# Expert weights of a routed FFN loaded, split and released in half chunks, with six half buffers for three whole ones

## The chip, the cores and the metric

The kernel runs on one core of a Trainium2 chip, as one program. The metric is the time of one execution on the device in microseconds, the median of several runs. The engines are named as the profile names them: PE is TensorE (PEld its weight loads), DVE is VectorE, ACT is ScalarE, POOL is GpSimd, SP is SyncE, which here only issues DMAs.

## What is computed

One layer of an encoder on 1024 tokens of width 1024, all in float32: a mixing sub-layer (a Fourier branch and attention, gated and projected), then a feed-forward sub-layer in which a router sends each token to 4 of 32 experts, each with a normalising residual. The change lies in the second sub-layer. Cut to what matters, the reference does this there:

```python
logits = xf @ w_router + b_router                   # 1024 tokens, 32 experts
top_vals, top_idx = lax.top_k(logits, 4)
top_w = softmax(top_vals)
# for each expert e and each of its tokens:
h = xb @ w_gate_up[e] + b_gate_up[e]                # 1024 -> 2048
gate = minimum(h[:, :1024], 7.0); up = clip(h[:, 1024:], -7.0, 7.0)
act = (up + 1.0) * gate * sigmoid(1.702 * gate)
y = act @ w_down[e] + b_down[e]                     # 1024 -> 1024
# y times the token's weight is added to the token's row of the output
```

The weights of the 32 experts, 12 MiB each, are read once.

## The kernel before

Up to about 1047 us of the profile the kernel computes the mixing sub-layer, the norm and the router, and ranks the experts by their number of tokens. The expert stage then works through all 32 experts by rank. Each rank has a fixed capacity in tokens (CAPS, from 416 down to 64); tokens beyond it would go through a loop at the end (the pool `pvw`), which uses the same loader.

Float32 products are made of float32r matmuls: a weight is split into `whi`, its rounded value (ACT, line 147), and `wlo`, the rest (DVE, line 148), and the tokens' values are split the same way. A product takes three matmuls (hi by hi, lo by hi, hi by lo), or two where the tokens' two parts lie side by side in one matmul.

**Chunks.** An expert's weights come in 12 chunks of 1 MiB: eight of gate and up (`G1`, chunks 0 to 7: four groups of 256 columns of each, in two halves of the contraction) and four of down (`G2`, chunks 8 to 11). `load_chunk` (line 994) takes a `wraw` tile of 128 x 2048 floats, lets SP issue its loads (two DMAs of 512 KB for gate and up, line 1003; one of 1 MiB for down, line 1005 for experts with few tokens, 1007 for the popular ones), and splits the tile in two halves of 1024 columns (`HALVES`, line 1012) into one `whi` and one `wlo` tile. The pool `pew` has three buffers of each kind. `Stream.get` hands out the next chunk and asks for loads two chunks ahead.

**Lanes.** The 14 popular ranks (over 128 tokens) form lane a, the other 18 lane b. `moe_plan` merges the steps of both lanes into one list by a cost of each step and a rest behind some, and the program is written out in this order; the framework then builds every engine's queue from it ahead of the run with a simulated timeline, so matmuls of neighbouring steps may be interleaved, and the queues are then fixed.

- Lane a keeps weights as the stationary operand (`cols`, line 1108 and on): a pair of chunks (h = 0, 1) fills four PSUM tiles `psg`, indexed by j (128 columns of the group) and t (gate or up). For each of the four in turn the k steps of the chunk run (lines 1124 to 1128). After the second chunk each j is evicted (`gu`, lines 1137 to 1141), put through the activation (lines 1143 to 1146), and split into `aTa` (lines 1152 and 1153), the moving operand of the down chunks (`down_mm`, lines 1203 and 1204, or the three of `mm3`, lines 141 to 143). Results are weighted (`weigh`, line 1215) and scattered to the tokens' rows by POOL.
- Lane b keeps the tokens stationary (`rows`, lines 1164 to 1169): a pair of chunks accumulates into one PSUM tile `psr`; the result is turned (`at`, line 1189) for the down chunks.

While an expert runs, POOL gathers the rows of the next expert of its lane, and PE turns them (line 1088) in between its down chunks; the table of rows that the gather needs is loaded by SP during the second chunk. The first steps also add the down bias to the output (`bias_out`, lines 1256 to 1259).

Of the kernel before, what the change touches and what calls it, by code (L numbers as in the profile page):

```python
# [12 lines left out]
F32 = mybir.dt.float32  # L13
# [10 lines left out]
P = 128  # L24
# [13 lines left out]
CAPS = [416, 320, 288, 288, 256, 256, 240, 208, 208, 192, 192, 160, 160, 160] + 7 * [128] + 11 * [64]  # L38

RANK_AT = 6  # L40
HALVES = [(0, 4), (4, 8)]
N_BIG = sum(n > P for n in CAPS)
LANE_A = [9, 0, 4, 1, 5, 2, 6, 3, 7, 8, 10, 11, 12, 13]
LANE_B = list(range(NE - 1, N_BIG - 1, -1))
# [62 lines left out]
def layer_kernel(ctx, tc, x, c, w_ada, b_ada, w_in, q_norm_g, k_norm_g, w_fourier, w_attn_o, w_out,  # L107
# [886 lines left out]
    def load_chunk(pl, wgu, wdn, i, wide=True, after=None):  # L994


        raw = pl.tile([P, KT, 256], F32, name="wraw")
        c, h = divmod(i % 8, 2)
        ks = slice(4 * h, 4 * h + 4)
        if i in G1:  # L1000
            rv = raw.rearrange("p (k t) f -> p k t f", t=2)
            for t in range(2):
                sp.dma_start(rv[:, :, t, :], wgu[:, ks, t, c * 256:(c + 1) * 256])
        elif wide:
            sp.dma_start(raw.rearrange("p (k t) f -> p k (t f)", t=2), wdn[:, ks, c * 512:(c + 1) * 512])
        else:
            sp.dma_start(raw, wdn[:, :, (i - 8) * 256:(i - 7) * 256])
        hi = pl.tile([P, KT, 256], F32R, name="whi")
        lo = pl.tile([P, KT, 256], F32R, name="wlo")
        with tc.issue_after(after.ins) if after else nullcontext():  # L1010
            for a, b in HALVES:
                split(raw[:, a:b, :], hi[:, a:b, :], lo[:, a:b, :])
        if i in G1 or wide:
            return tuple(w.rearrange("p (k t) f -> p k (t f)", t=2) for w in (hi, lo))
        return hi, lo

    def weights_of(e):
        return (w_gate_up[0][bass.ds(e, 1)].rearrange("o (k p) (t f) -> p (o k) t f", p=P, t=2),
# [8 lines left out]
        vec.tensor_tensor(a_, a_, gu[:n, 1, :], op=ALU.mult)  # L1027

    plan = moe_plan()
    with tc.tile_pool(name="pew", bufs=3, side=RIGHT) as pew, tc.tile_pool(name="pes", bufs=1, side=RIGHT) as pes, \  # L1030
# [27 lines left out]
        class Expert:  # L1058
# [49 lines left out]
            def cols(self, i):  # L1108

                n, xT, aT, r = self.n, self.xT, self.aT, self.r  # L1110
                merged = n < 256
                c, h = divmod(i, 2)
                wh, wl = wst.get()
                if h == 0:
                    self.pg = [[peg.tile([P, 512], F32, name="psg") for t in range(2)] for j in range(2)]
                for j in range(2):
                    for t in range(2):
                        ps = self.pg[j][t]
                        cs = slice(t * 256 + j * P, t * 256 + (j + 1) * P)
                        for k in range(4):  # L1120
                            first, last = h == 0 and k == 0, h == 1 and k == 3
                            xh, xl = xT[:, 4 * h + k, 0, :], xT[:, 4 * h + k, 1, :]
                            if merged:
                                pe_.matmul(ps[:, :2 * n], wh[:, k, cs], xT[:, 4 * h + k, :, :], start=first, stop=False)  # L1124
                            else:
                                pe_.matmul(ps[:, :n], wh[:, k, cs], xh, start=first, stop=False)  # L1126
                                pe_.matmul(ps[:, :n], wh[:, k, cs], xl, start=False, stop=False)  # L1127
                            pe_.matmul(ps[:, :n], wl[:, k, cs], xh, start=False, stop=last)  # L1128
                    if h == 0:
                        continue  # L1130
                    ft = 2 * c + j
                    gu = pe.tile([P, 2, n], F32, name="gu", bufs=1)
                    for t, lim in ((0, LIMIT), (1, LIMIT + 1.0)):
                        ps = self.pg[j][t]
                        bb = BG[:, 8 * t + ft, r:r + 1]
                        if merged:
                            act.activation(gu[:, t, :], ps[:, n:2 * n], AF.Identity, bias=bb)
                            vec.tensor_tensor(gu[:, t, :], ps[:, :n], gu[:, t, :], op=ALU.add)
                            vec.tensor_scalar(gu[:, t, :], gu[:, t, :], lim, None, op0=ALU.min)
                        else:  # L1140
                            vec.tensor_scalar(gu[:, t, :], ps[:, :n], bb, lim, op0=ALU.add, op1=ALU.min)
                    sg = pe.tile([P, n], F32, name="sgg", bufs=1)
                    act.activation(sg, gu[:, 0, :], AF.Sigmoid, scale=SLOPE)
                    vec.scalar_tensor_tensor(gu[:, 1, :], gu[:, 1, :], 1.0 - LIMIT, gu[:, 0, :], op0=ALU.max,
                                             op1=ALU.mult)
                    vec.tensor_tensor(sg, gu[:, 1, :], sg, op=ALU.mult)
                    nf = n // P
                    for b0, nb_, m in ((0, nf, P), (nf * P, 1, n - nf * P)):
                        if nb_ and m:
                            av = aT[:, ft, 2 * b0:2 * (b0 + nb_ * m)].rearrange("p (b t q) -> p b t q", b=nb_, t=2)  # L1150
                            sv = sg[:, b0:b0 + nb_ * m].rearrange("p (b q) -> p b q", b=nb_)
                            act.activation(av[:, :, 0, :], sv, AF.Copy)  # L1152
                            vec.tensor_tensor(av[:, :, 1, :], sv, f32(av)[:, :, 0, :], op=ALU.subtract)  # L1153

            def rows(self, i):
# [5 lines left out]
                wh, wl = wst.get()  # L1161
                o = self.ps[:m, :]
                if h == 0:
                    pe_.matmul(o, self.sel[:, :m], b2v[:, :, c * 256:(c + 1) * 256], start=True, stop=False)
                for k in range(4):
                    xk, last = xT[:, 4 * h + k, :, :], h == 1 and k == 3
                    if m > n:
                        pe_.matmul(o, xk, wh[:, k, :], start=False, stop=False)  # L1168
                        pe_.matmul(o, xk, wl[:, k, :], start=False, stop=last)  # L1169
                    else:  # L1170
                        mm3(o, xk[:, 0, :], xk[:, 1, :], wh[:, k, :], wl[:, k, :], False, last)
                if h == 0:
                    return
                pv = self.ps.rearrange("p (t f) -> p t f", t=2)
# [18 lines left out]
            def down_mm(self, o, b0, m, w, k0, first, last):  # L1193

                aT = self.aT
                wh, wl = w
                hs, ls = slice(2 * b0, 2 * b0 + m), slice(2 * b0 + m, 2 * (b0 + m))
                bs = slice(2 * b0, 2 * (b0 + m))
                nk = wh.shape[1]
                for k in range(nk):  # L1200
                    f_, l_ = first and k == 0, last and k == nk - 1
                    if m in (32, 64):
                        pe_.matmul(o[:2 * m], aT[:, k0 + k, bs], wh[:, k, :], start=f_, stop=False)
                        pe_.matmul(o[:2 * m], aT[:, k0 + k, bs], wl[:, k, :], start=False, stop=l_)
                    else:
                        mm3(o[:m], aT[:, k0 + k, hs], aT[:, k0 + k, ls], wh[:, k, :], wl[:, k, :], f_, l_)

            def weigh(self, o, m, wt, y, cs):

# [127 lines left out]
                e.chunk(i, [partial(nx.xt, *bh) for bh in halves])  # L1337


    with tc.tile_pool(name="pv", bufs=1) as pv, tc.tile_pool(name="pvw", bufs=3) as pvw, \  # L1340
            tc.tile_pool(name="pvp", bufs=2, space=PSUM) as pvp:
        nov = nc.values_load(novi[0:1, 0:1], min_val=0, max_val=NB_MAX)
        with tc.For_i(0, nov, 1) as bi:  # L1343
# [32 lines left out]
            for c in range(4):  # L1376
                ps = pvp.tile([P, 512], F32, name="vps")
                pe_.matmul(ps, eb, b2v[:, :, c * 256:(c + 1) * 256], start=True, stop=False)
                for h in range(2):
                    wh, wl = ws3.get()  # L1380
                    for k in range(4):
                        xk = xT[:, 4 * h + k, :, :]
                        mm3(ps, xk[:, 0, :], xk[:, 1, :], wh[:, k, :], wl[:, k, :], False, h == 1 and k == 3)
                gu = pv.tile([P, 2, 256], F32, name="vgu", bufs=2)
                swiglu(gu, ps.rearrange("p (t f) -> p t f", t=2), P, av[:, c * 256:(c + 1) * 256])
            aT = columns(av, "vaT")
            y = pv.tile([P, D], F32, name="vy")
            for c in range(2):
                ps = pvp.tile([P, 512], F32, name="vps")
                for h in range(2):  # L1390
                    wh, wl = ws3.get()
                    for k in range(4):
                        ak = aT[:, 4 * h + k, :, :]
                        mm3(ps, ak[:, 0, :], ak[:, 1, :], wh[:, k, :], wl[:, k, :], h == 0 and k == 0,
                            h == 1 and k == 3)
# [85 lines left out]
```

## Time and profile before

| | |
|---|---|
| median of 3 runs | 2810.29 us (2807.48 to 2818.73) |
| the profiled execution | 2809.73 us |
| its span, first to last instruction | 2808.0 us |
| mean granted TensorE clock | 0.952 of full |
| PE busy (x instructions) | 2544.5 us, 91% (x15948) |
| DVE busy | 2083.0 us, 74% (x3672) |
| ACT busy | 1421.8 us, 51% (x2190) |
| POOL busy | 380.1 us, 14% (x283) |
| moved by DMA | 561.23 MB, mean 200 GB/s |

Busy shares over the whole span are a mean over stages that differ: the expert stage takes from 1047 to 2740 us. The rows further down are from this stage. A group's row gives the instructions of one line and tile: their busy time, the mean of one in ns, and behind the bar the idle time of the engine just ahead of them with what ended it. Matmuls are pipelined, so the mean of one is longer than the step from one to the next. The duration of an SP row is that of issuing, not of the transfer.

### The profile page before, as it was taken

Reading aid. Unit: us, or ns where it says so; the run is one execution under the profiler, and the core shown is the slowest. Engines: PE = TensorE matmul, PEld = TensorE weight load, DVE = VectorE, ACT = ScalarE, POOL = GpSimd, SP = SyncE. Lnnn points to the kernel's source line nnn. Section 1 sums busy time; section 2 is a strip of 40 time slices with the busy share of each in tenths; the row PEclk is TensorE's granted clock in tenths of the full one; section 3 lists DMA queues with packets and bytes.
Section 4 is the critical chain, followed back from the end, with each engine's and each line's share of the span. In section 5 each row is a group of like instructions: output and inputs, shape, how many; then the busy total and the mean of one; then the engine's idle time right before and its main releaser. Section 6 shows DMA issues by size and latency. Waiting matters only on the chain. (4 is left out here: it accounts for less than half of the span.)

```text
span 2808.0 us, 43022 instructions
## 1 busy us (share of the span) xinstructions
PE 2544.5 (91%) x15948; PEld 2307.1 (82%) x15948; DVE 2083.0 (74%) x3672; ACT 1421.8 (51%) x2190; POOL 380.1 (14%) x283
## 2 busy tenths in 40 slices
PE   6999999899999947889989989989999999998991
PEld 5888899799888946789889888977888888897881
DVE  7543438777755956868788888969896888887885
ACT  3411122466621535645566556647665665665562
POOL 3100012211032232000201010011101010020003
PEclk9999999999999958999999999999999999999996
DMA  6154411000054349857889799978988898988774
GB/s 229 55 185 158 160 55 31 16 1 1 1 179 145 121 150 259 250 173 251 255 273 290 239 292 282 301 230 276 287 282 247 273 295 272 290 285 257 248 250 152
DMA packets 468742, 561.23 MB, mean 200 GB/s; under 512 B 26632, under 2 KB 404944, under 8 KB 468480
## 3 DMA queue, kind: packets, MB, share of 16 engines
q1 hardware_dynamic: 448672, 494.41, 53.9%
q0 software_dynamic: 18768, 59.64, 8.4%
q10 hardware_dynamic: 1088, 4.39, 0.5%
q8 instruction: 127, 2.08, 0.3%
q14 instruction: 87, 0.71, 0.1%
HBM read 512.90 MB, written 46.82 MB: 199 GB/s over the span
## 5 line engine op out<-in xcount | busy, mean ns | idle before, releaser
L148 DVE TENSOR_TENSOR wlo<-wraw,whi 128x1024 fp32r<-128x1024 f32 x768 | 909.7, 1217 | 220.1 <-ACT whi L147 216.0
L147 ACT ACTIVATE whi<-wraw 128x1024 fp32r<-128x1024 f32 x768 | 767.9, 1051 | 462.8 <-DMA wraw<-in_w_gate_up_dram 130.7
L1128 PE MATMUL psg<-xTa,wlo 128*128 128x160 f32 (+7 forms) x1792 | 469.5, 278 | 3.1 <-DVE wlo L148 3.0
L1128 PEld LDWEIGHTS psg<-xTa,wlo 128*128 128x128 f32 x1792 | 341.6, 194 | 8.4 <-DVE wlo L148 6.1
L1124 PE MATMUL psg<-xTa,whi 128*128 128x320 f32 (+3 forms) x1024 | 307.1, 367 | 12.4 <-ACT whi L147 10.7
L141 PE MATMUL psd<-whi,aTa 128*128 128x256 f32 (+2 forms) x768 | 220.6, 291 | 27.1 <-ACT aTa L1152 17.6
L1126 PE MATMUL psg<-xTa,whi 128*128 128x256 f32 (+3 forms) x768 | 233.3, 308 | 11.3 <-ACT whi L147 9.1
L1127 PE MATMUL psg<-xTa,whi 128*128 128x256 f32 (+3 forms) x768 | 231.9, 305 | 0.0
L143 PE MATMUL psd<-whi,aTa 128*128 128x256 f32 (+2 forms) x768 | 216.8, 287 | 3.5 <-DVE aTa L1153 3.3
L142 PE MATMUL psd<-wlo,aTa 128*128 128x256 f32 (+2 forms) x768 | 217.5, 285 | 0.1
L1124 PEld LDWEIGHTS psg<-xTa,whi 128*128 128x128 f32 x1024 | 195.8, 194 | 23.5 <-ACT whi L147 13.2
L141 PEld LDWEIGHTS psd<-whi,aTa 128*128 128x128 f32 (+2 forms) x768 | 145.7, 190 | 36.1 <-ACT aTa L1152 21.2
L1126 PEld LDWEIGHTS psg<-xTa,whi 128*128 128x128 f32 x768 | 147.4, 192 | 14.9 <-ACT whi L147 10.8
L991 POOL DMA_INDIRECT acc_d<-xya,tab x33 | 60.6, 1836 | 654.0 <-DVE xya L1215 544.2
L143 PEld LDWEIGHTS psd<-whi,aTa 128*128 128x128 f32 (+2 forms) x768 | 145.0, 190 | 5.0 <-DVE aTa L1153 4.4
L1127 PEld LDWEIGHTS psg<-xTa,whi 128*128 128x128 f32 x768 | 147.5, 192 | 1.3
L1169 PE MATMUL psr<-wlo,xTb 128*128 128x512 f32 x352 | 145.1, 412 | 3.2 <-DVE wlo L148 3.1
L142 PEld LDWEIGHTS psd<-wlo,aTa 128*128 128x128 f32 (+2 forms) x768 | 145.9, 190 | 1.3 <-DVE wlo L148 0.4
L1168 PE MATMUL psr<-whi,xTb 128*128 128x512 f32 x352 | 144.6, 411 | 2.4 <-ACT whi L147 2.4
L147 ACT ACTIVATE wh<-wraw 128x1024 fp32r<-128x1024 f32 (+1 forms) x35 | 48.1, 1377 | 154.4 <-PE psg L206 92.9
L152 ACT ACTIVATE pth<-pst 128x512 fp32r<-128x512 f32 x128 | 75.1, 599 | 86.4 <-PE pst L632 85.1
L141 PE MATMUL pz<-wh,uh 128*128 128x256 f32 x384 | 110.4, 288 | 2.4 <-DVE mrow L480 2.4
(455 smaller groups left out, 6407.5 us busy)
## 6 DMA issues: line engine op xcount, KB each, us to landing
wraw<-in_w_gate_up_dram SPq DMA_DIRECT2D x512, 512.0 KB
wraw<-in_w_down_dram SPq DMA_DIRECT2D x128, 1024.0 KB
wa<-in_w_ada_dram SPq DMA_DIRECT2D x24, 1024.0 KB
wraw<-in_w_in_dram SPq DMA_DIRECT2D x13, 1024.0 KB
xs<-in_x_dram SPq DMA_DIRECT2D x8, 512.0 KB
m_d<-sgm POOLq DMA_DIRECT2D x8, 512.0 KB, 4.1
sa_d<-sgm POOLq DMA_DIRECT2D x8, 512.0 KB, 2.9
wraw<-in_w_attn_o_dram SPq DMA_DIRECT2D x8, 512.0 KB
```

The costliest lines, as they stand in the source:

```text
L141: pe_.matmul(o, lh, rh, start=start, stop=False)
L142: pe_.matmul(o, lh, rl, start=False, stop=False)
L143: pe_.matmul(o, ll, rh, start=False, stop=stop)
L147: act.activation(hi, raw, AF.Copy)
L148: (lo_eng or vec).tensor_tensor(lo, raw, f32(hi), op=ALU.subtract)
L152: act.activation(hi, ps, AF.Copy)
L1124: pe_.matmul(ps[:, :2 * n], wh[:, k, cs], xT[:, 4 * h + k, :, :], start=first, stop=False)
L1126: pe_.matmul(ps[:, :n], wh[:, k, cs], xh, start=first, stop=False)
L1127: pe_.matmul(ps[:, :n], wh[:, k, cs], xl, start=False, stop=False)
L1128: pe_.matmul(ps[:, :n], wl[:, k, cs], xh, start=False, stop=last)
L1168: pe_.matmul(o, xk, wh[:, k, :], start=False, stop=False)
L1169: pe_.matmul(o, xk, wl[:, k, :], start=False, stop=last)
```

## The change

`load_chunk` now makes two half chunks of a chunk. Each has its own `wraw`, `whi` and `wlo` tile of 128 x 1024 floats, its own loads (of two k steps of gate and up, or of half the rows of a down chunk) and its own split, and the pool has six buffers of each kind, so that the bytes stay the same. A chunk is now a list of two pairs. `rows`, `down_mm` and the overflow loop index the right half for each k; their order of matmuls is the same. `cols` runs both k steps of the first half for all four `psg` tiles, then those of the second; the evictions follow after all of it.

```diff
     def load_chunk(pl, wgu, wdn, i, wide=True, after=None):
-        raw = pl.tile([P, KT, 256], F32, name="wraw")
         c, h = divmod(i % 8, 2)
-        ks = slice(4 * h, 4 * h + 4)
-        if i in G1:
-            rv = raw.rearrange("p (k t) f -> p k t f", t=2)
-            for t in range(2):
-                sp.dma_start(rv[:, :, t, :], wgu[:, ks, t, c * 256:(c + 1) * 256])
-        elif wide:
-            sp.dma_start(raw.rearrange("p (k t) f -> p k (t f)", t=2), wdn[:, ks, c * 512:(c + 1) * 512])
-        else:
-            sp.dma_start(raw, wdn[:, :, (i - 8) * 256:(i - 7) * 256])
-        hi = pl.tile([P, KT, 256], F32R, name="whi")
-        lo = pl.tile([P, KT, 256], F32R, name="wlo")
-        with tc.issue_after(after.ins) if after else nullcontext():
-            for a, b in HALVES:
-                split(raw[:, a:b, :], hi[:, a:b, :], lo[:, a:b, :])
-        if i in G1 or wide:
-            return tuple(w.rearrange("p (k t) f -> p k (t f)", t=2) for w in (hi, lo))
-        return hi, lo
+        out_ = []
+        for q in range(2):
+            raw = pl.tile([P, 4, 256], F32, name="wraw")
+            ks = slice(4 * h + 2 * q, 4 * h + 2 * q + 2)
+            if i in G1:
+                rv = raw.rearrange("p (k t) f -> p k t f", t=2)
+                for t in range(2):
+                    sp.dma_start(rv[:, :, t, :], wgu[:, ks, t, c * 256:(c + 1) * 256])
+            elif wide:
+                sp.dma_start(raw.rearrange("p (k t) f -> p k (t f)", t=2), wdn[:, ks, c * 512:(c + 1) * 512])
+            else:
+                sp.dma_start(raw, wdn[:, 4 * q:4 * q + 4, (i - 8) * 256:(i - 7) * 256])
+            hi = pl.tile([P, 4, 256], F32R, name="whi")
+            lo = pl.tile([P, 4, 256], F32R, name="wlo")
+            with tc.issue_after(after.ins) if after else nullcontext():
+                split(raw, hi, lo)
+            if i in G1 or wide:
+                hi, lo = (w.rearrange("p (k t) f -> p k (t f)", t=2) for w in (hi, lo))
+            out_.append((hi, lo))
+        return out_
...
-    with tc.tile_pool(name="pew", bufs=3, side=RIGHT) as pew, ...
+    with tc.tile_pool(name="pew", bufs=6, side=RIGHT) as pew, ...
...
-                wh, wl = wst.get()
+                ws = wst.get()
...
-                for j in range(2):
-                    for t in range(2):
+                for q, (wh, wl) in enumerate(ws):
+                    for j, t in ((j, t) for j in range(2) for t in range(2)):
                         ps = self.pg[j][t]
                         cs = slice(t * 256 + j * P, t * 256 + (j + 1) * P)
-                        for k in range(4):
-                            first, last = h == 0 and k == 0, h == 1 and k == 3
-                            xh, xl = xT[:, 4 * h + k, 0, :], xT[:, 4 * h + k, 1, :]
+                        for k in range(2):
+                            kk = 4 * h + 2 * q + k
+                            first, last = kk == 0, kk == KT - 1
+                            xh, xl = xT[:, kk, 0, :], xT[:, kk, 1, :]
...
+                for j in range(2):
                     if h == 0:
                         continue
                     ft = 2 * c + j
...
                 for k in range(4):
+                    wh, wl = (w[:, k % 2, :] for w in ws[k // 2])
                     xk, last = xT[:, 4 * h + k, :, :], h == 1 and k == 3
```

## Rows read from the trace of the kernel before

**Rows 1.** Table by stage: engines' busy us, granted clock, DMA share, GB/s.
```profile
1047.00:1247.00 200.00, 163.99 (x852) 145.97 (x853) 137.40 (x253) 109.97 (x173) 29.54 (x26) 0.89 0.77 229
1247.00:2740.00 1493.00, 1405.32 (x8968) 1286.89 (x8967) 1248.60 (x2026) 910.29 (x1358) 144.10 (x86) 0.97 0.85 268
```
**Rows 2.** Groups from 1247 to 2740 us: the splits on DVE and ACT.
```profile
L148 DVE TENSOR_TENSOR wlo<-wraw,whi 128x1024 fp32r<-128x1024 f32 x692 | 820.1, 1217 | 181.1 <-ACT whi L147 177.2 <-PE psg L1128 2.0 <-PE psd L143 0.7
...
L147 ACT ACTIVATE whi<-wraw 128x1024 fp32r<-128x1024 f32 x692 | 692.2, 1051 | 413.9 <-DMA wraw<-in_w_gate_up_dram 125.7 <-PE psd L1203 63.7 <-PE psr L143 59.6
```
**Rows 3.** Groups from 1247 to 2740 us: PE's matmuls with idle ahead.
```profile
L1128 PE MATMUL psg<-xTa,wlo 128*128 128x160 f32 (+7 forms) x1600 | 414.9, 276 | 1.5 <-DVE wlo L148 1.4
L1124 PE MATMUL psg<-xTa,whi 128*128 128x320 f32 (+3 forms) x896 | 265.9, 365 | 8.5 <-ACT whi L147 8.1 <-DVE gu L1138 0.4
L1126 PE MATMUL psg<-xTa,whi 128*128 128x256 f32 (+3 forms) x704 | 210.6, 303 | 9.1 <-ACT whi L147 9.1
...
L141 PE MATMUL psd<-whi,aTa 128*128 128x256 f32 (+2 forms) x720 | 206.1, 290 | 25.4 <-ACT aTa L1152 15.9 <-DVE xya L1215 6.2 <-DVE xya L1212 2.9
...
L143 PE MATMUL psd<-whi,aTa 128*128 128x256 f32 (+2 forms) x720 | 202.9, 286 | 3.3 <-DVE aTa L1153 3.3
L1169 PE MATMUL psr<-wlo,xTb 128*128 128x512 f32 x288 | 116.0, 403 | 2.0 <-DVE wlo L148 1.9
L1168 PE MATMUL psr<-whi,xTb 128*128 128x512 f32 x288 | 115.1, 400 | 1.2 <-ACT whi L147 1.2
L142 PE MATMUL psr<-wlo,xTb 128*128 128x512 f32 x224 | 89.3, 398 | 2.8 <-DVE wlo L148 2.7
L141 PE MATMUL psr<-whi,xTb 128*128 128x512 f32 x224 | 89.1, 398 | 1.4 <-ACT whi L147 1.3
...
L1203 PE MATMUL psr<-whi,aTb 128*128 128x512 f32 x160 | 64.9, 406 | 5.1 <-ACT whi L147 4.4 <-DVE xyb L1212 0.5 <-DVE gu L1138 0.2
...
L141 PE MATMUL psr<-whi,aTb 128*128 128x512 f32 x112 | 44.9, 400 | 2.2 <-ACT whi L147 2.2
```
**Rows 4.** ACT's waits from 1247 to 2740 us: us in total, times, longest.
```profile
ACT whi L147 <- DMA wraw<-in_w_gate_up_dram: 125.7, 83, 7.6
...
ACT whi L147 <- DMA wraw<-in_w_down_dram: 22.3, 18, 2.1
```
**Rows 5.** Timelines of DVE, SP and ACT: start, duration, instruction, idle before.
```profile
1917.04 2.36 DVE L148 TENSOR_TENSOR wlo<-wraw,whi 128x1024 fp32r<-128x1024 f32 x2 [1.23 <-ACT whi L147]
...
1919.43 0.94 SPq L1003 DMA_DIRECT2D wraw<-in_w_gate_up_dram  x2
...
1924.82 2.00 ACT L147 ACTIVATE whi<-wraw 128x1024 fp32r<-128x1024 f32 x2 [0.67 <-DMA wraw<-in_w_gate_up_dram]
...
1926.57 2.34 DVE L148 TENSOR_TENSOR wlo<-wraw,whi 128x1024 fp32r<-128x1024 f32 x2
...
1928.94 0.37 SPq L1005 DMA_DIRECT2D wraw<-in_w_down_dram  x1
```
**Rows 6.** Table by stage again, two stretches of 50 us.
```profile
2147.00:2197.00 50.00, 46.42 (x246) 41.01 (x244) 43.45 (x77) 33.06 (x53) 3.51 (x2) 0.97 0.97 317
2297.00:2347.00 50.00, 50.00 (x290) 45.27 (x289) 46.26 (x78) 34.73 (x56) 4.45 (x2) 1.00 0.99 317
```
**Rows 7.** SP's load instructions by line: count, ns min/median/max; the page's sizes.
```profile
L1005 SPq DMA_DIRECT2D wraw<-in_w_down_dram x72: 372/373/377, 1110.0 to 2724.3; - x72
...
wraw<-in_w_gate_up_dram SPq DMA_DIRECT2D x512, 512.0 KB
wraw<-in_w_down_dram SPq DMA_DIRECT2D x128, 1024.0 KB
```
**Rows 8.** Timelines of PE and DVE around one pass of the popular lane.
```profile
2180.71 0.54 PE L1124 MATMUL psg<-xTa,whi 128*128 128x416 f32 x2
...
2183.11 0.41 PE L1164 MATMUL psr<-b,sel 128*128 128x512 f32 x1
...
2183.45 0.65 DVE L1138 TENSOR_TENSOR gu<-psg,gu 128x208 f32<-128x208 f32 x2
...
2186.35 0.35 PE L1124 MATMUL psg<-xTa,whi 128*128 128x416 f32 x1
```

More of the change, by code (lines that the diff above doesn't have):

```diff
@@ L40 @@
 RANK_AT = 6
-HALVES = [(0, 4), (4, 8)]
 N_BIG = sum(n > P for n in CAPS)
@@ L1029, in layer_kernel @@
     plan = moe_plan()
-    with tc.tile_pool(name="pew", bufs=3, side=RIGHT) as pew, tc.tile_pool(name="pes", bufs=1, side=RIGHT) as pes, \
+    with tc.tile_pool(name="pew", bufs=6, side=RIGHT) as pew, tc.tile_pool(name="pes", bufs=1, side=RIGHT) as pes, \
             tc.tile_pool(name="pe", bufs=2) as pe, \
@@ L1112, in cols @@
                 c, h = divmod(i, 2)
-                wh, wl = wst.get()
+                ws = wst.get()
                 if h == 0:
                     self.pg = [[peg.tile([P, 512], F32, name="psg") for t in range(2)] for j in range(2)]
-                for j in range(2):
-                    for t in range(2):
+                for q, (wh, wl) in enumerate(ws):
+                    for j, t in ((j, t) for j in range(2) for t in range(2)):
                         ps = self.pg[j][t]
                         cs = slice(t * 256 + j * P, t * 256 + (j + 1) * P)
-                        for k in range(4):
-                            first, last = h == 0 and k == 0, h == 1 and k == 3
-                            xh, xl = xT[:, 4 * h + k, 0, :], xT[:, 4 * h + k, 1, :]
+                        for k in range(2):
+                            kk = 4 * h + 2 * q + k
+                            first, last = kk == 0, kk == KT - 1
+                            xh, xl = xT[:, kk, 0, :], xT[:, kk, 1, :]
                             if merged:
-                                pe_.matmul(ps[:, :2 * n], wh[:, k, cs], xT[:, 4 * h + k, :, :], start=first, stop=False)
+                                pe_.matmul(ps[:, :2 * n], wh[:, k, cs], xT[:, kk, :, :], start=first, stop=False)
                             else:
@@ L1160, in rows @@
                     self.ps = pep.tile([P, 512], F32, name="psr", bufs=1)
-                wh, wl = wst.get()
+                ws = wst.get()
                 o = self.ps[:m, :]
@@ L1165, in rows @@
                 for k in range(4):
+                    wh, wl = (w[:, k % 2, :] for w in ws[k // 2])
                     xk, last = xT[:, 4 * h + k, :, :], h == 1 and k == 3
                     if m > n:
-                        pe_.matmul(o, xk, wh[:, k, :], start=False, stop=False)
-                        pe_.matmul(o, xk, wl[:, k, :], start=False, stop=last)
+                        pe_.matmul(o, xk, wh, start=False, stop=False)
+                        pe_.matmul(o, xk, wl, start=False, stop=last)
                     else:
-                        mm3(o, xk[:, 0, :], xk[:, 1, :], wh[:, k, :], wl[:, k, :], False, last)
+                        mm3(o, xk[:, 0, :], xk[:, 1, :], wh, wl, False, last)
                 if h == 0:
@@ L1195, in down_mm @@
                 aT = self.aT
-                wh, wl = w
                 hs, ls = slice(2 * b0, 2 * b0 + m), slice(2 * b0 + m, 2 * (b0 + m))
                 bs = slice(2 * b0, 2 * (b0 + m))
-                nk = wh.shape[1]
+                nq = w[0][0].shape[1]
+                nk = 2 * nq
                 for k in range(nk):
+                    wh, wl = (a[:, k % nq, :] for a in w[k // nq])
                     f_, l_ = first and k == 0, last and k == nk - 1
                     if m in (32, 64):
-                        pe_.matmul(o[:2 * m], aT[:, k0 + k, bs], wh[:, k, :], start=f_, stop=False)
-                        pe_.matmul(o[:2 * m], aT[:, k0 + k, bs], wl[:, k, :], start=False, stop=l_)
+                        pe_.matmul(o[:2 * m], aT[:, k0 + k, bs], wh, start=f_, stop=False)
+                        pe_.matmul(o[:2 * m], aT[:, k0 + k, bs], wl, start=False, stop=l_)
                     else:
-                        mm3(o[:m], aT[:, k0 + k, hs], aT[:, k0 + k, ls], wh[:, k, :], wl[:, k, :], f_, l_)
+                        mm3(o[:m], aT[:, k0 + k, hs], aT[:, k0 + k, ls], wh, wl, f_, l_)
             def weigh(self, o, m, wt, y, cs):
@@ L1337, in layer_kernel @@
                 e.chunk(i, [partial(nx.xt, *bh) for bh in halves])
-    with tc.tile_pool(name="pv", bufs=1) as pv, tc.tile_pool(name="pvw", bufs=3) as pvw, \
+    with tc.tile_pool(name="pv", bufs=1) as pv, tc.tile_pool(name="pvw", bufs=6) as pvw, \
             tc.tile_pool(name="pvp", bufs=2, space=PSUM) as pvp:
@@ L1379, in layer_kernel @@
                 for h in range(2):
-                    wh, wl = ws3.get()
+                    w = ws3.get()
                     for k in range(4):
+                        wh, wl = (a[:, k % 2, :] for a in w[k // 2])
                         xk = xT[:, 4 * h + k, :, :]
-                        mm3(ps, xk[:, 0, :], xk[:, 1, :], wh[:, k, :], wl[:, k, :], False, h == 1 and k == 3)
+                        mm3(ps, xk[:, 0, :], xk[:, 1, :], wh, wl, False, h == 1 and k == 3)
                 gu = pv.tile([P, 2, 256], F32, name="vgu", bufs=2)
@@ L1390, in layer_kernel @@
                 for h in range(2):
-                    wh, wl = ws3.get()
+                    w = ws3.get()
                     for k in range(4):
+                        wh, wl = (a[:, k % 2, :] for a in w[k // 2])
                         ak = aT[:, 4 * h + k, :, :]
-                        mm3(ps, ak[:, 0, :], ak[:, 1, :], wh[:, k, :], wl[:, k, :], h == 0 and k == 0,
-                            h == 1 and k == 3)
+                        mm3(ps, ak[:, 0, :], ak[:, 1, :], wh, wl, h == 0 and k == 0, h == 1 and k == 3)
                 cs = slice(c * 512, (c + 1) * 512)
```

## The prediction

> **What bounds the kernel now.** I read the page's busy shares first, then the table by stage, the groups of instructions inside the long stage, the waits, and last the timeline of a few loads.
>
> The stage table [rows 1] gives the expert stage three parts. From 1047 to 1247 us it starts up: TensorE (PE) is busy 164.0 of 200 us. From 1247 to 2740 us it runs steadily: PE 1405.3 of 1493 us, so PE idles 87.7 us; VectorE (DVE) is busy 1248.6 us, ScalarE (ACT) 910.3 us, the DMA engines 0.85 of the time. Behind 2740 us comes the closing norm. The change touches the first two parts alone. No engine is full: PE leads at 94%, DVE has 84%, DMA 85%. Three carriers so close together lose time to each other through finite buffers, and buffers are what the change alters.
>
> Two groups show how heavy the weight path is [rows 2]: rounding and subtracting are 692 instructions each, 1.05 us on ACT and 1.22 us on DVE. ACT idles 413.9 us ahead of its roundings, the largest idle of that engine, and 148.0 us of that end with a load's landing, in 101 waits [rows 4]. The rest ends with PE, which had still to read an older whi buffer.
>
> On PE itself [rows 3] the waits for whi are 8.1 + 9.1 + 1.2 + 1.3 + 4.4 + 2.2 = 26.3 us and for wlo 1.4 + 1.9 + 2.7 = 6.0 us: 32 us of the 87.7 wait for weights directly. The largest single wait is another one, 15.9 us for aTa. But aTa and the evictions stand in ACT's and DVE's queues behind those same roundings and subtractions, so a late load delays them too.
>
> The timeline shows the ring of buffers at work [rows 5]. The two subtractions of one chunk run on DVE from 1917.04 to 1919.40; SP issues the load that reuses the buffer at 1919.43, at once. ACT starts on that load at 1924.82, a wait that the landing ended, 5.4 us after the issue. Its subtractions end at 1928.91 and SP reissues at 1928.94. A raw buffer thus lives 9.5 us here, with three of them 3.2 us a chunk. In the busiest stretches the engines move 317 GB/s at a DMA share of 0.97 to 0.99 [rows 6]; 1 MiB takes 3.3 us at that rate. So in such stretches ring and wire are equally tight.
>
> **The change part by part.** The count and size of ACT's, DVE's and PE's instructions stay: splits were already made by halves of 1024 columns. Buffers hold the same bytes.
>
> Loads and release by halves. The first half's load can be issued when the first subtraction ends, one DVE instruction (1.2 us) earlier than now. It lands after half the bytes, 1.65 us at 317 GB/s instead of 3.3. So the first rounding can start up to 1.2 + 1.65 = 2.9 us earlier where a load is what it waits for, and the second half, issued when the whole chunk is now, follows behind only 1.65 us of its own bytes: 1.65 us earlier, with its sibling already rounded. The waits for loads average 148.0 / 101 = 1.5 us, so most could vanish. Releasing whi and wlo by halves helps the other 266 us of ACT's idle: a rounding needs only the first half of the older buffer read, which comes half a chunk of matmuls earlier. What of this PE sees lies between nothing (another queue is late at once) and all 87.7 us; the direct waits are 32 us. I take half, 44 us, nearer to the direct waits than to the whole, since aTa and the evictions queue behind the splits only in part. The first 200 us I leave as they are.
>
> Clock. The granted clock is 0.97 in the steady part [rows 1], which is 0.03 x 1493 = 45 us of full-speed work lost at the low level (1.2 of 2.4 GHz). It is lower, 0.89, in the start-up, where PE idles more. Halving the idle could return between 0 and half of the 45; I take 10.
>
> DMA instructions. Gate and up loads go from two to four a chunk, down loads from one to two: 640 more instructions of 0.37 us on SP [rows 7], 239 us in all, over 1690 us in which SP otherwise waits. They wait on SP for DVE as the loads do now; the table loads of the next expert queue behind them, but those are made a whole expert ahead. The two issues of a half follow its release as the two of a chunk do now (0.94 us for both, rows 5), so the path gets no longer: 0. Should that cover go, 0.37 us on each of the 101 awaited loads would be 37 us.
>
> Here a rule speaks against the change. The rows move 317 GB/s with loads that are mostly 512 KB [rows 6, 7]. The Trainium skill (DMA: Bandwidth & Descriptors, section Bandwidth) says to batch DMAs to 1 MiB or more for 75% of peak, so by it quarter-MiB loads would lose rate; the trace, at 317 GB/s from half of that size, does not show the loss, since several loads are queued at a time. Its consequence here is the third rival.
>
> Matmul order in the popular lane. Now each of the four psg tiles gets its four k steps in turn; then two k steps go to all four tiles, and the other two follow. Two effects. A starved chunk can do half its matmuls before it needs the second half: part of the 44. Against that, tile (1,0) of the next pair is needed after a quarter of a chunk instead of half. One pass shows how near that lies [rows 8]: it starts at 2180.71, its first two tiles last to 2183.11, and the third is evicted by DVE from 2183.45 to 2184.10 only; the order built into PE's queue fills the time with matmuls of the other lane and returns at 2186.35. A quarter is 1.2 us there. Evictions of the first pair also begin later (its last matmul moves from one half of the second pass to three quarters), which pushes the second pair's post-processing back and with it aTa at the start of the down chunks. Lower end 0, since today's waits for gu are 0.4 us and the order fills such holes. Upper end: by the kernel's own plan 16 of 56 such borders have at most 0.5 us of the other lane between them, 16 x 1.2 = 19 us, and the 19.2 us now waited for aTa (15.9 + 3.3) might double: 38 us. I take 14, about a third, nearer to the rows of today.
>
> Sum, against the profiled execution (2809.7 us, its span 2808.0, and the median of the runs 2810.3, so no correction): 2809.7 - 44 - 10 + 0 + 14 = 2770 us.
>
> **The rivals.** First, the waits only move. DVE is busy 84% and DMA 85% of the steady part; in stretches like 2147 to 2197 the wire is full [rows 6], and an earlier issue then only queues longer. For it: PE's largest wait is for aTa. Against it: the ring reissues at once, so the wire does idle in between (DMA 0.85 on average against 0.99). Only some 10 us of the direct 32 would be won and 4 lost to the order: 2804 us.
>
> Second, slower: the matmul order makes evictions late. All 56 borders then cost a quarter, 56 x 1.2 = 67 us, against the 44 gained: 2833 us. It decides where DVE evicts the second pair more than a quarter of a chunk after the next pass began and nothing ready can be put between. Rows 8 show such an eviction, and also the filling.
>
> Third, slower: each transfer has a part that is not bytes. In rows 5 it is 5.4 - 3.3 = 2.1 us; if the second half paid it anew without overlap, less the 1.2 us of earlier issue, 101 waits would grow by 0.9 us, 91 us on ACT; PE sees 87.7 of ACT's 413.9 us today, a fifth: 19 us, 2829 us. This is what the page's rule would do here; the rate of rows 6 speaks against it.
>
> That the halves do nothing at all, because the built order of the queues is rearranged around them, is part of the first.
>
> **How the numbers follow.** The forecast gets 0.55, with a range of its own from 2722 (all 88 us won, without the clock) to 2796; the first rival 0.23, the second 0.15, the third 0.07. The far ends are 2809.7 - 88 - 22 = 2700 and 2809.7 + 38 = 2848. For 8 in 10 I take 2722 to 2826: past the first rival and up to the third's time less a little. Half a percent, 14 us, is about what a measurement of this kernel can tell from no change. The forecast's cases lie beyond it (0.55, and 0.01 of the first rival's); the first rival lies within it (0.22); the second and third are slower (0.22).
>
> **What would show it.** Right: ACT's idle ahead of whi falls well below 414 us, above all the part that loads end; DMA share above 0.85 between 1247 us and a stage end near 2700; PE idle near 44 us; subtraction and reissue one by one instead of in pairs. The first rival: DMA share the same, ACT's waits ended by PE instead. The second: PE waits for gu grow from 0.4 us to tens, and aTa's too. The third: fewer GB/s in the busiest stretches than 317. The forecast fails if the order that is built into the queues changes in other places than these.

## The result: 2743.4 us, 2.35% faster

| | before | changed |
|---|---|---|
| median | 2808.9 us (2802.5 to 2818.7, 4 runs) | 2743.4 us (2737.7 to 2745.7, 4 runs) |
| ratio | 1 | 0.9765, 95% interval 0.9741 to 0.9788 |
| profiled execution | 2809.7 us, span 2808.0 us | 2745.7 us, span 2743.9 us |

The forecast was 2770 us with a range of 2722 to 2826: the time lies inside, and 65.5 us were won instead of 40. Some terms behind that number were wrong nevertheless, one of them in sign, and the experiments tell which.

In the changed kernel the split stands on lines 146 (ACT) and 147 (DVE), loads on 1004 (gate and up), 1006 and 1008 (down), the matmuls of the popular lane on 1126 to 1130. The table by stage of the changed kernel answers to [rows 1]; columns are the stretch, its length, then PE, PEld, DVE, ACT and POOL busy, the granted clock, the DMA share and GB/s:

```profile
1047.00:1247.00 200.00, 172.80 (x903) 155.24 (x903) 144.82 (x261) 116.53 (x180) 26.44 (x26) 0.90 0.82 239
1247.00:2675.00 1428.00, 1368.00 (x8898) 1258.28 (x8897) 1242.77 (x2017) 922.52 (x1350) 139.49 (x86) 0.99 0.90 279
```

The steady part ends at 2675 us, 65 us sooner than the 2740 of before, so all of the gain lies up to there; the mixing sub-layer ahead of 1047 us did not move. PE's idle went from 36.0 to 27.2 us in the start-up and from 87.7 to 60.0 us in the steady part. The granted clock rose from 0.97 to 0.99 there: 0.03 x 1493 = 45 us of lost full-speed work became 0.01 x 1428 = 14 us. Together 9 + 28 + 31 us, and 2 us of clock in the start-up (0.11 x 200 against 0.10 x 200), make 70 us; the profiled executions differ by 64. The clock of a stretch is printed to a hundredth, which leaves some 7 us either way in each of the steady figures. The page of the whole execution is sharper; its line of busy times in the changed kernel:

```profile
PE 2519.7 (92%) x15948; PEld 2290.9 (83%) x15948; DVE 2082.3 (76%) x3672; ACT 1440.9 (53%) x2190; POOL 372.0 (14%) x283
```

PE's busy time for the same 15948 matmuls fell from 2544.5 to 2519.7 us, by 25 us, and its idle (span less busy) from 263.5 to 224.2 us, by 39 us. The mean granted clock of the whole execution, 0.952 before and 0.960 now, gives the same 25 us: 0.048 x 2808.0 = 135 us lost at the low level became 0.040 x 2743.9 = 110 us.

The groups of the splits and ACT's waits from 1247 to 2675 us answer to [rows 2] and [rows 4]:

```profile
L146 ACT ACTIVATE whi<-wraw 128x1024 fp32r<-128x1024 f32 x687 | 709.9, 1055 | 354.7 <-DMA wraw<-in_w_gate_up_dram 81.0 <-PE psr L142 60.6 <-PE psg L1129 45.5
```
```profile
ACT whi L146 <- DMA wraw<-in_w_gate_up_dram: 81.0, 77, 4.0
ACT whi L146 <- PE psr L142: 60.6, 80, 3.0
```

Waits for gate and up loads fell from 125.7 to 81.0 us, the longest from 7.6 to 4.0 us, and those for down loads from 22.3 to 9.8 us. These 57 us are nearly all that ACT's idle ahead of its roundings lost (413.9 to 354.7 us); the rest of that idle stayed, 266 us before and 264 us now. PE's own groups, beside [rows 3]:

```profile
L1126 PE MATMUL psg<-xTa,whi 128*128 128x320 f32 (+3 forms) x896 | 261.0, 360 | 6.3 <-DVE gu L1141 4.9 <-ACT whi L146 1.4
L140 PE MATMUL psd<-whi,aTa 128*128 128x256 f32 (+2 forms) x715 | 201.1, 284 | 13.7 <-DVE xya L1220 7.6 <-ACT aTa L1155 4.3 <-DVE xya L1217 1.8
L1128 PE MATMUL psg<-xTa,whi 128*128 128x256 f32 (+3 forms) x688 | 199.4, 297 | 2.3 <-DVE gu L1144 2.2
L142 PE MATMUL psd<-whi,aTa 128*128 128x256 f32 (+2 forms) x714 | 197.7, 281 | 2.0 <-DVE aTa L1156 2.0
L1167 PE MATMUL psr<-b,sel 128*128 128x512 f32 x64 | 28.5, 446 | 19.1 <-DVE xyb L1217 7.9 <-DVE gur L1182 6.6 <-DVE gur L1025 3.6
```

Waits for whi on the large groups of the popular lane are down from 8.1 + 9.1 us to 1.4 us and nothing. Waits for evicted psg tiles (gu) are up, but only from 0.4 to 4.9 + 2.2 = 7.1 us, and as much with the old order of matmuls (e1 below). Those for aTa are down from 15.9 + 3.3 to 4.3 + 2.0 us where a rise was feared. What is late now is lane b's turn-over, 19 us (6.7 us before) ahead of the first matmul of a psr tile.

The timelines show the ring by halves, beside [rows 5]: one subtraction ends at 1864.17 + 1.23 = 1865.40 and SP issues the two loads of one half at 1865.42; the next ends at 1867.44, with issues from 1867.46.

```profile
1864.17 1.23 DVE L147 TENSOR_TENSOR wlo<-wraw,whi 128x1024 fp32r<-128x1024 f32 x1
...
1866.23 1.21 DVE L147 TENSOR_TENSOR wlo<-wraw,whi 128x1024 fp32r<-128x1024 f32 x1
```
```profile
1865.42 0.95 SPq L1004 DMA_DIRECT2D wraw<-in_w_gate_up_dram  x2
```

### The profile page after: what moved, and what is told of

Read it like the earlier page. It is cut to its first block, busy times and chain, and to the rows that moved or that the text cites. A ratio compares the mean times of both kernels' runs of the same rounds, so it can differ in the third digit from the quotient of the medians.

```text
span 2743.9 us, 46418 instructions
## 1 busy us (share of the span) xinstructions
PE 2519.7 (92%) x15948; PEld 2290.9 (83%) x15948; DVE 2082.3 (76%) x3672; ACT 1440.9 (53%) x2190; POOL 372.0 (14%) x283
## 3 DMA queue, kind: packets, MB, share of 16 engines
HBM read 512.90 MB, written 46.82 MB: 204 GB/s over the span
## 5 line engine op out<-in xcount | busy, mean ns | idle before, releaser
L147 DVE TENSOR_TENSOR wlo<-wraw,whi 128x1024 fp32r<-128x1024 f32 x768 | 921.3, 1217 | 177.7 <-ACT whi L146 161.7
L146 ACT ACTIVATE whi<-wraw 128x1024 fp32r<-128x1024 f32 x768 | 793.7, 1055 | 406.2 <-DMA wraw<-in_w_gate_up_dram 90.9
L140 PE MATMUL psd<-whi,aTa 128*128 128x256 f32 (+2 forms) x768 | 217.6, 286 | 15.8 <-DVE xya L1220 7.6
L1129 PE MATMUL psg<-xTa,whi 128*128 128x256 f32 (+3 forms) x768 | 229.3, 302 | 0.0
L1128 PE MATMUL psg<-xTa,whi 128*128 128x256 f32 (+3 forms) x768 | 226.6, 303 | 2.3 <-DVE gu L1144 2.2
L142 PE MATMUL psd<-whi,aTa 128*128 128x256 f32 (+2 forms) x768 | 214.1, 282 | 3.6 <-DVE aTa L1156 3.6
L1126 PEld LDWEIGHTS psg<-xTa,whi 128*128 128x128 f32 x1024 | 193.7, 193 | 24.9 <-issue 9.1
L140 PEld LDWEIGHTS psd<-whi,aTa 128*128 128x128 f32 (+2 forms) x768 | 142.3, 186 | 22.0 <-DVE xya L1220 9.7
L1128 PEld LDWEIGHTS psg<-xTa,whi 128*128 128x128 f32 x768 | 143.9, 188 | 5.7 <-ACT whi L146 2.0
L1129 PEld LDWEIGHTS psg<-xTa,whi 128*128 128x128 f32 x768 | 144.7, 188 | 1.4
L142 PEld LDWEIGHTS psd<-whi,aTa 128*128 128x128 f32 (+2 forms) x768 | 141.9, 186 | 4.7 <-DVE aTa L1156 4.5
```

Of the source, the lines that this page charges most:

```text
L140: pe_.matmul(o, lh, rh, start=start, stop=False)
L142: pe_.matmul(o, ll, rh, start=False, stop=stop)
L146: act.activation(hi, raw, AF.Copy)
L147: (lo_eng or vec).tensor_tensor(lo, raw, f32(hi), op=ALU.subtract)
L1126: pe_.matmul(ps[:, :2 * n], wh[:, k, cs], xT[:, kk, :, :], start=first, stop=False)
```

## The experiments

Four parts can be told apart: wraw by halves (loads and release), whi and wlo by halves (release), the order of matmuls, and the size of the loads alone. All times are set against runs of the kernel before on the same chip. PE idle and clock are of the expert stage, from 1047 us to 55 us ahead of the span's end (length less busy, read from the table by stage), and "loads" is ACT's wait ahead of whi that landings of gate, up and down loads ended, in the same stretch. These three columns are read from one profiled execution of each kernel, which can lie off the median (2765.7 us in e3, 2805.7 us in e6), so a few us more or less in them say little.

| kernel | median us | ratio, 95% interval | PE idle us | clock | loads us |
|---|---|---|---|---|---|
| before | 2808.9 | 1 | 125.2 | 0.96 | 150.8 |
| loads halved only (e5) | 2803.3 | 0.9967 to 0.9994 | 121.4 | 0.97 | 146.8 |
| order only (e10) | 2814.3 | 0.9998 to 1.0028 | 130.9 | 0.97 | 144.3 |
| wraw by halves (e2) | 2796.0 | 0.9940 to 0.9972 | 115.7 | 0.97 | 112.6 |
| whi by halves (e6) | 2797.7 | 0.9949 to 0.9983 | 121.4 | 0.96 | 182.5 |
| wlo by halves (e7) | 2803.2 | 0.9961 to 1.0003 | 114.6 | 0.96 | 153.8 |
| whi, wlo by halves (e3) | 2773.4 | 0.9850 to 0.9902 | 105.2 | 0.98 | 162.2 |
| the same, new order (e11) | 2772.4 | 0.9855 to 0.9902 | 105.6 | 0.98 | 152.4 |
| all by halves, old order (e1) | 2756.8 | 0.9784 to 0.9841 | 97.4 | 0.98 | 94.5 |
| new order in first chunks (e8) | 2748.8 | 0.9774 to 0.9814 | 87.8 | 0.98 | 78.7 |
| the change | 2743.4 | 0.9741 to 0.9788 | 87.2 | 0.98 | 95.2 |
| buffers 4, 7, 7 (e9) | 2881.8 | 1.0249 to 1.0295 | 162.6 | 0.95 | 367.3 |
| buffers 7, 6, 5 (e12) | 2731.1 | 0.9709 to 0.9760 | 78.0 | 0.98 | 88.3 |
| buffers 8, 5, 5 (e13) | 2720.6 | 0.9673 to 0.9724 | 70.2 | 0.98 | 38.9 |

### All by halves, old order (e1)

The theory after the result was still that of the prediction: the ring of loads carries the gain and the order costs.

```diff
-                for q, (wh, wl) in enumerate(ws):
-                    for j, t in ((j, t) for j in range(2) for t in range(2)):
+                for j, t in ((j, t) for j in range(2) for t in range(2)):
+                    for q, (wh, wl) in enumerate(ws):
```

> The change with the matmuls of the popular lane in their old order (each psg tile takes all four k steps of a chunk in turn). Theory (the loads, splits and releases by halves carry the gain, the new order costs 14 us through late evictions): about 2730 us, between 2720 and 2738, and PE's waits for gu back near 0.4 us. Rival (the new order carries part of the gain, since it frees the first half of whi after half a chunk): 2755 to 2775 us, with more idle of ACT ended by PE's psg matmuls.

It took 2756.8 us, in the rival's range. The new order gains some 13 us on top of the halves; it does not cost 14. The two intervals of the table just touch, but every run of e1 (2751.7 to 2760.1 us) is slower than every run of the change.

Neither sign came as told. PE's waits for gu did not go back to 0.4 us: from 1247 to 2686 us they are 4.7 + 2.7 us, so it is not the new order that made them grow:

```profile
L1126 PE MATMUL psg<-xTa,whi 128*128 128x320 f32 (+3 forms) x896 | 262.3, 361 | 5.9 <-DVE gu L1141 4.7 <-ACT whi L146 1.1
L1128 PE MATMUL psg<-xTa,whi 128*128 128x256 f32 (+3 forms) x688 | 201.3, 298 | 8.2 <-ACT xTa L151 4.3 <-DVE gu L1144 2.7 <-ACT whi L146 1.1
```

And ACT's idle ahead of whi that psg matmuls ended is no longer than in the change (89 against 98 us over the stage). What the order gains is 10 us of PE idle, in several waits at once, the largest share for lane b's gur (20.2 us in e1, 13.7 us in the change). How the order shortens them stays open.

### wraw by halves alone (e2)

```diff
+        hi = pl.tile([P, KT, 256], F32R, name="whi")
+        lo = pl.tile([P, KT, 256], F32R, name="wlo")
+        for q in range(2):
+            raw = pl.tile([P, 4, 256], F32, name="wraw", bufs=6)
+            ks = slice(4 * h + 2 * q, 4 * h + 2 * q + 2)
...
+                split(raw, hi[:, a:b, :], lo[:, a:b, :])
```

> Only wraw comes in halves (six half buffers, loads of half chunks, each released by its own subtraction); whi and wlo stay whole with three buffers, old order of matmuls. Theory (the ring of raw buffers, reissued earlier and landing earlier, carries most): 2760 to 2780 us, with ACT's idle ended by loads down by half, that ended by PE as before. Rival (the release of whi by halves carries it): 2800 us or more.

2796.0 us: 13 us won, less than the theory's 30 to 50. The mechanism is there, since waits ended by loads fell from 150.8 to 112.6 us, by a quarter where half was foretold, and those ended by PE stayed as they were (285 and 291 us). But before, too, loads ended only a third of ACT's idle ahead of its roundings (150.8 of 459.2 us).

### whi and wlo by halves alone (e3)

```diff
-        hi = pl.tile([P, KT, 256], F32R, name="whi")
-        lo = pl.tile([P, KT, 256], F32R, name="wlo")
+        for q in range(2):
+            hi = pl.tile([P, 4, 256], F32R, name="whi")
+            lo = pl.tile([P, 4, 256], F32R, name="wlo")
...
+                split(raw[:, 4 * q:4 * q + 4, :], hi, lo)
```

> Only whi and wlo come in halves (six half buffers); wraw stays whole with three buffers and whole loads, old order of matmuls. Theory: the raw ring still binds, 2790 to 2808 us, ACT's idle ended by loads stays near 148 us in the steady part. Rival (release of whi carries it): 2760 to 2780 us, ACT's idle ended by PE down by a third or more.

2773.4 us: 36 us, the rival's time, over half of the whole gain and with no load changed. Its second sign came weakly: the part of ACT's idle that PE ended fell from 285 to 249 us, an eighth and not a third. As waits ended by loads rose a little (150.8 to 162.2 us), ACT's whole idle hardly moved (444 us in its group, after 459). PE's idle shrank by 20 us, and the granted clock rose with it.

### Half loads into whole tiles (e5)

```diff
+        for q in range(2):
+            ks = slice(4 * h + 2 * q, 4 * h + 2 * q + 2)
+            rq = raw[:, 4 * q:4 * q + 4, :]
...
+                    sp.dma_start(rv[:, :, t, :], wgu[:, ks, t, c * 256:(c + 1) * 256])
```

> The kernel before with each load split into two half loads into the same whole wraw tile: twice the DMA instructions, half the size, no earlier release. Theory (a transfer has next to no fixed part on the path, and the first half lands earlier, so the first rounding starts earlier): 2795 to 2808 us. Rival (each transfer pays a fixed part anew): 2820 us or more, with fewer than 317 GB/s in the busiest stretches.

2803.3 us, the theory's range: twice the instructions at half the size cost nothing and win perhaps 5 us. The third rival of the prediction falls, and its sign is missing: the fastest stretch of 50 us moves no less than the 317 GB/s of [rows 6], in e5 (first row) and in the changed kernel (second), both with gate and up loads of 256 KB:

```profile
2147.00:2197.00 50.00, 47.77 (x265) 42.59 (x265) 44.83 (x81) 34.51 (x56) 1.10 (x1) 1.00 1.00 322
2097.00:2147.00 50.00, 47.78 (x258) 42.40 (x257) 43.69 (x73) 33.36 (x50) 8.55 (x6) 1.00 1.08 333
```

The 2.1 us besides the bytes that the prediction read in [rows 5] were mostly time behind the load ahead. ACT had waited for that one too:

```profile
1921.84 2.01 ACT L147 ACTIVATE whi<-wraw 128x1024 fp32r<-128x1024 f32 x2 [0.50 <-DMA wraw<-in_w_gate_up_dram]
```

The next landing let ACT start at 1924.82, 2.98 us later, which is less than the 3.3 us of 1 MiB at 317 GB/s.

The Trainium skill (DMA: Bandwidth & Descriptors, section Bandwidth) asks for 1 MiB or more per DMA. No run here shows a loss below that size: with several loads on their way at once, the fastest stretch went from 317 to 333 GB/s.

### whi alone and wlo alone (e6, e7)

In e6 wlo is one whole tile again, in e7 whi is; the loads and wraw stay whole in both.

```diff
+        whole = pl.tile([P, KT, 256], F32R, name="wlo", bufs=3)
...
-            lo = pl.tile([P, 4, 256], F32R, name="wlo")
+            lo = whole[:, 4 * q:4 * q + 4, :]
```

> Only whi comes in halves (six half buffers); wlo and wraw stay whole with three buffers, old order of matmuls. With whi and wlo both in halves the time was 2773 us, 36 us under the kernel before. Theory A (ACT's rounding waits for PE to let go of whi, and an earlier release of its first half lets everything behind it go earlier): most of the gain, 2775 to 2790 us. Theory B (the gain needs wlo too, since the subtraction of a half waits for the whole old wlo and raw is released by the subtraction): 2795 us or more.

> Only wlo comes in halves (six half buffers); whi and wraw stay whole with three buffers, old order of matmuls. Theory A: little or nothing, 2800 to 2810 us, since the rounding ahead of the subtraction still waits for the whole old whi. Theory B: a third of the 36 us or more, under 2797 us.

2797.7 and 2803.2 us: 10 and 4 us (the interval of e7 reaches no change at all), and together, in e3, 36. Neither theory holds alone; what holds of B is that the two pay far more together than apart. In e6 the wait moved one engine on. ACT could round sooner, and DVE then stood before a whole wlo that PE still read. DVE's waits in e6 from 1247 to 2690 us (us in total, times, longest):

```profile
DVE wlo L147 <- ACT whi L146: 140.3, 107, 5.5
...
DVE wlo L147 <- PE psr L141: 15.6, 13, 3.8
...
DVE wlo L147 <- PE psd L141: 5.5, 2, 2.8
```

In the kernel before, waits of wlo for PE come to 2.0 + 0.7 us [rows 2]. And as a raw buffer is let go by the subtraction, waits for loads rose to 182.5 us.

### The order by chunk, and alone (e8, e10, e11)

e8 takes the new order for the first chunk of a pair and the old for the second; e10 puts the new order on the kernel before; e11 puts it on e3.

```diff
+                parts = [(q, j, t) for q in range(2) for j in range(2) for t in range(2)] if h == 0 else \
+                    [(q, j, t) for j in range(2) for t in range(2) for q in range(2)]
```

> The change, but with the new matmul order in the first chunk of each pair alone; the second chunk has the old order, so evictions of the first tiles can begin after half of it again. The new order in both gave 2743 us, the old in both 2757 us. Theory (starting on the first half is worth over 14 us, and late evictions cost some of it back): 2730 to 2741 us. Rival (evictions cost nothing, the gain of the order comes from freeing the first half of whi, in both chunks alike): about 2750 us, half way.

2748.8 us, half way between 2756.8 and 2743.4, as the rival had it, though with intervals that overlap on both sides. If late evictions cost anything worth seeing, giving up the new order in the chunk that they follow would have won.

> The kernel before with the new matmul order alone: whole chunks, whole tiles, three buffers. The prediction's step (the order itself costs through late evictions): 2815 to 2825 us. Theory now (the order gained 13 us on half tiles because it frees and starts on halves; with whole tiles nothing is freed sooner, and evictions cost next to nothing): 2802 to 2812 us. Rival (the gain is in starting on the first half, whoever releases): 2790 to 2800 us.

2814.3 us, with an interval from nothing to 0.28% slower. That lies between the 2802 to 2812 of the theory and the 2815 to 2825 of the prediction's step: no clear cost, and no gain either.

> whi and wlo in halves (six half buffers) with the new order, wraw whole with three buffers and whole loads: the change less its part on the loads. With the old order it was 2773 us. Theory (the order frees the first halves sooner, whatever the loads do): 2757 to 2766 us. Rival (the loads bind there, so the order brings nothing): 2770 to 2778 us.

2772.4 against 2773.4 us: with whole loads the order brings nothing. So it pays only where wraw comes in halves too. A reason would be that the order lets go of first halves sooner, and that this is worth something only where the half load that follows has landed. No run shows it: waits for loads are the same with either order, 94.5 us in e1 and 95.2 us in the change.

### The same bytes shared out otherwise (e9, e12, e13)

```diff
-            raw = pl.tile([P, 4, 256], F32, name="wraw")
+            raw = pl.tile([P, 4, 256], F32, name="wraw", bufs=8)
...
-            hi = pl.tile([P, 4, 256], F32R, name="whi")
-            lo = pl.tile([P, 4, 256], F32R, name="wlo")
+            hi = pl.tile([P, 4, 256], F32R, name="whi", bufs=5)
+            lo = pl.tile([P, 4, 256], F32R, name="wlo", bufs=5)
```

> The change with the same bytes shared out otherwise: four half buffers of wraw, seven of whi and of wlo. Theory (whi and wlo held by PE are what the splits wait for, the raw ring is the lesser limit): 2730 to 2743 us, ACT's idle ended by PE well under 230 us in the steady part. Rival (raw binds as soon as it has fewer buffers): 2760 us or more, with more idle of ACT ended by loads.

2881.8 us: 74 us slower than the kernel before. One buffer more of whi and of wlo does not make up for two fewer of wraw, and ACT's waits show why:

```profile
ACT whi L146 <- DMA wraw<-in_w_gate_up_dram: 281.6, 247, 6.9
ACT whi L146 <- DMA wraw<-in_w_down_dram: 85.7, 90, 2.6
```

> The change with the same bytes shared out otherwise: seven half buffers of wraw, six of whi, five of wlo. With four, seven and seven it was 2882 us. Theory (a missing raw buffer is the dearer one, and wlo, written last and freed with whi, can spare one): 2730 to 2743 us, ACT's idle ended by loads under 90 us. Rival (whi and wlo only gain together, so the shorter of the two limits both): 2755 us or more, with more idle ended by PE.

> The change with eight half buffers of wraw, five of whi and five of wlo. Six, six and six gave 2743 us, seven, six and five 2731 us, four, seven and seven 2882 us. If wraw is still the limit: 2715 to 2730 us. If whi, which PE holds, binds once it has fewer than three chunks: 2740 us or more, with over 230 us of ACT's idle ended by PE in the steady part.

2731.1 and 2720.6 us, both in the range that makes wraw the limit. The last is faster than the change: its interval (0.9673 to 0.9724) ends below that of the change (0.9741 to 0.9788). Each set against its own runs of the kernel before, it wins 19 us more than the change (84 against 65.5 us). Its stage and ACT's group, from 1047 to 2662 us:

```profile
1047.00:2662.00 1615.00, 1544.85 (x9898) 1422.03 (x9898) 1390.08 (x2285) 1034.86 (x1530) 205.11 (x113) 0.98 0.89 276
```
```profile
L146 ACT ACTIVATE whi<-wraw 128x1024 fp32r<-128x1024 f32 x760 | 782.0, 1055 | 397.2 <-PE psg L1129 83.0 <-PE psr L142 79.8 <-PE psd L1208 60.4
```

ACT's idle is as long as in the change (397.2 against 400.2 us over the same stage), but loads end only 38.9 us of it, PE nearly all the rest (330 us, of which 294 us lie in the steady part). Over 230 us there were to be the sign of a time of 2740 us or more; the time fell all the same. So between these two kernels time went with the waits that loads end, and not with those that PE ends. That is no rule: in e3 the waits that loads end rose, those that PE ends fell, and 36 us were won. And since buffers of one kind were traded for those of another, no run tells what one buffer of each kind is worth by itself.

## Why the prediction held, and where it was wrong

**What bounds the kernel.** Right: finite buffers between carriers of much the same load. Every kernel of the table reads the same 512.90 MB and runs the same 15948 matmuls, and the times lie from 2721 to 2882 us.

**Loads and release by halves, 44 us.** The mechanism is right, the size was too high. The term counts PE idle, and by that the halves alone, with the old order, are worth 28 us over the stage (125.2 to 97.4, e1). That the net came out near, 28 us in the steady part and 9 in the start-up that was left as it is, against 44 less 14 for the order, is luck: the order gave 10 us of idle where 14 were charged, so two errors went opposite ways. The split inside the term was wrong too. The prediction worked it out from the loads (2.9 us earlier) and named the release of whi and wlo as a help; in time, and with the old order, the loads and wraw alone bring 13 us, whi and wlo alone 36 us, both 52 us. Nor did the 266 us of ACT's other idle, which the release was to help, get shorter in the change (264 us).

**Clock, 10 us.** The other mis-sized term: about 25 us, by PE's busy time for the same matmuls. The 10 us were not worked out from a row, since no row of before shows how the clock answers to shorter gaps. In the table the two go together: kernels with over 110 us of PE idle have 0.95 to 0.97, those with 106 us or less 0.98. Small changes of idle show no such return: in e2, e5, e6 and e7 PE's idle over the whole span fell by 6 to 11 us and its busy time moved by about 2 us at most. No run changes the gaps alone, so what in them moves the clock stays open.

**DMA instructions, 0.** Right (e5).

**Matmul order, 14 us of cost.** Wrong in sign with everything in halves: 13 us of gain (e1). Waits for gu did grow, to 7.1 us, but to 7.4 us in e1 with the old order too, so the order did not cause it. aTa's, which were to double, shrank by 13 us. That the built order of PE's queue had other matmuls for the holes, as in [rows 8], fits this, but no run shows it. Alone, the order does between nothing and 0.28% of harm (e10). The step that failed is the upper end drawn from a quarter of a chunk at 16 borders and from aTa's waits doubled, of which I took a third. Rows 8 spoke for taking nothing.

**The rivals.** The first (waits only move) describes e6 well, where one wait took the place of another, but not the change. The second fell with e1 and e8, the third with e5.

**Signs.** Seen: reissue half by half, DMA share up from 0.85 to 0.90, the steady part's end at 2675 us, and less of ACT's idle ahead of whi ended by loads (148.0 to 90.8 us). Seen in part: that idle as a whole (354.7 us after 413.9, and 400.2 us after 459.2 over the whole stage), which mixes waits for loads with waits for PE. Not seen: PE idle near 44 us in the steady part; it is 60.0 us.

Left open: the framework rebuilds every engine's queue for each of these kernels, so a difference holds the shorter waits and the changed order together. That the parts add up, 13 + 36 against 52 us, speaks for the waits; no run held the order fixed. What rebuilding alone can do may be judged by e5 and e10, which lie within 6 us of the kernel before; the 10 and 4 us of e6 and e7 are hardly more.

## What to carry to other kernels

Where load, split and use form a chain with few buffers, cut all links of it to the same grain. whi and wlo, which are made one behind the other, won 10 and 4 us when one alone was cut and 36 us together: in e6, with whi alone cut, part of the wait passed on to wlo. The loads and wraw added their 13 us to that, and all together gave 52 us without another byte of memory. Then try how the memory is shared out: 8, 5 and 5 halves in place of three times 6 won 19 us more, while 4, 7 and 7 lost the whole gain and 74 us besides. And price idle time of TensorE above its length where much of it can go, since here 39 us less idle came with 25 us less busy time for the same matmuls.

## What the runs showed of the hardware

The granted clock returned nearly two thirds of what the idle itself gave, which I had not expected in a stage where PE is busy 94% of the time: with 39 us less idle, the same matmuls took 25 us less (mean clock 0.952 to 0.960). In e13 it was 60 us of idle and 31 us of busy time.

The 317 GB/s at a DMA share of 0.97 to 0.99, which the prediction took for a full wire [rows 6], were not its limit: the change moves 333 GB/s and e13 348 GB/s (1347 to 1397 us), both at a share of 1.08.

And SP waited more for older loads to land before it could issue, though this cost nothing that shows; the row is of the change from 1247 to 2675 us:

```profile
SPq L1004 <- DMA wraw<-in_w_gate_up_dram: 45.1, 75, 2.2
```

Over the whole expert stage such waits were 16.9 us in 15 times before and are 52.7 us in 88 times in the change, and 67.2 us in 131 times in e13, with eight raw buffers, the fastest of all. They come with the halved loads and not with the halved buffers: e5, where only the loads were halved, has 44.9 us in 84 times, and e3, with whole loads, 13.8 us in 17 times. What holds SP there was not tried.
